# Two of the weight tiles of a Strassen product in the buffers of x, and the plain block second

## The chip, the cores and the metric

The kernel runs on one core of a Trainium2 chip. The time is device microseconds of one execution, and the median of several runs counts. The core has a matrix engine (TensorE, PE in the profile, with PEld for its loads of the stationary operand), a vector engine (VectorE, DVE), a scalar engine (ScalarE, ACT), a general engine (GpSimd, POOL) and a sequencer that here only issues transfers (SyncE, SP). Each engine works through its own list of instructions in order and waits on semaphores for the others. Transfers are issued from SP's list or from POOL's.

## The reference: what is computed

A decoder trunk of two layers on 256 tokens of width 1024, in float32. Each layer runs a SwiGLU, a token mixer and a second SwiGLU, each followed by a layer norm of `ALPHA * x + ...`. The four SwiGLUs are what matters here:

```
def _swiglu(x, w1, w3, w2):
    return (jax.nn.silu(x @ w1) * (x @ w3)) @ w2
...
        h = _swiglu(x, ffn_w1[l, 0], ffn_w3[l, 0], ffn_w2[l, 0])
        x = _layernorm(ALPHA * x + 0.5 * h, ln_g[l, 0], ln_b[l, 0])
```

The hidden width is 2816, so the last product, `h @ w2`, has 256 rows, 2816 terms and 1024 columns. There are four such products, the w2 stages of this text.

## The kernel before, in words

**Arithmetic.** Every float32 operand is split into a rounded part "hi" and the rest "lo" (ACT copies hi, DVE subtracts to get lo), and a product is three matmuls: hi by hi, hi by lo, lo by hi. Weights come from memory as raw float32 chunks of 128 x 2048 (1 MB) into a pool of four buffers (`raw_pool`, `RAW = 4`), are split in halves of 1024 columns into the pools `hi` and `lo` (eight buffers each), and are read by PE from there. `fetch` (its transfer is L161 of the profile) takes a raw buffer and issues the load on SP. `stream` is fetch and split (ACT L183, DVE L185); `split` is a split of its own (ACT L225, DVE L227).

**A SwiGLU.** `ffn` computes h in pieces. Blocks of 512 columns come in token order (`gemm_b2`), and each half is turned over by POOL's copies (L198), a transpose by DMA that SP issues (L202) and POOL's joining copies (L207); then ACT and DVE split it (L743, L745). Two column tiles come last in transposed order (`gemm_a2`, PE lines L261, L273 and L280). The input x lies in two tiles of a pool `xs` with two buffers; the last matmul that reads them is that of L280, just before the w2 stage. The norm behind the stage takes the same two buffers for the new x.

**The w2 stage** is `gemm_seven`. Of h, the first 8 of 22 column tiles form 2 x 2 blocks, and so do the matching rows of w2, in two column halves: w11, w21, w12, w22, each one chunk of 1 MB. This part is computed by a variant of Strassen's algorithm with seven block products; the names S1, S2 and so on in this text are the sums of weight blocks. The other 14 rows of tiles of w2 go through plain matmuls. `product` (PE L360) is one block product, 12 matmuls. `between` puts a group of 12 plain matmuls (PE L375) between two products; `rest` streams the chunks for it. The first column half is done in these groups; the second column half follows as a block behind them, first for the first 128 tokens, then for the others.

The sums of weight blocks are made in place. `plus` (DVE L344) adds a block to the raw tile r1: r1 = w11, then w11 + w12, then that + w22. `gather` (L339) lets a transfer of POOL's queue add a block from memory to a raw tile: to r2 (w12 + w22) and at the end to r1. So the raw tiles r1, r2 and, until its own product, r3 = w22 stay held while rest chunks and w21 come through the same pool. The results of the products are folded into the token rows `xtok` by DVE (`fold`, L573); two products share a bank with a fold in between, so the second has to wait for the fold.

**Order.** PE's list is written out by hand, in the order of the calls. For the other engines a planner orders the instructions by priority: `step()` in `fetch` and `gather` raises the number for what follows, and the planner can move an instruction that waits for a late one behind others. In its order of SP, the transposes of the last blocks of h stand among the loads of the w2 stage. `ffn` makes the object `Norm`, whose constructor asks for the norm's weights on POOL's queue (`bc_load`, L540) and, unless it is the last, for the two new x tiles.

Of the kernel before, what the change touches and what calls it, by code (L numbers as in the profile page):

```python
# [11 lines left out]
F32 = mybir.dt.float32  # L12
# [8 lines left out]
P = 128  # L21
# [15 lines left out]
CH = 2048  # L37
# [17 lines left out]
def trunk(ctx, tc, x, xT, w13a, w13b, w2, wb, wqk, wu, wg, wgr, wbr, wbrr, wo, gateb, gatebr, sgug, sgub, sguwT, sgubias, lam, diffg,  # L55
# [6 lines left out]
    raw_pool = ctx.enter_context(tc.tile_pool(name="raw", bufs=RAW))  # L62
    hi_pool = ctx.enter_context(tc.tile_pool(name="hi", bufs=HL))
    lo_pool = ctx.enter_context(tc.tile_pool(name="lo", bufs=HL))
    xs = ctx.enter_context(tc.tile_pool(name="xs", bufs=2))
# [8 lines left out]
    def name(s):  # L74
        serial[0] += 1
        return f"{s}_{serial[0]}"

    def bank():
        return psum.tile([P, 512], F32, tag="main", name=name("bank"))

    def side_bank():
        return psum.tile([P, 512], F32, tag="side", name=name("sbank"))
# [26 lines left out]
    def step():  # L109
        chunk[0] += 1  # L110
        tc.cur_priority = chunk[0] * STEP
# [12 lines left out]
    def beat(w):  # L124

        clock[0] += w
        for task in list(tasks):
            if task[0] <= clock[0]:
                turn(task)
# [18 lines left out]
    def behind(ins):  # L148

        return tc.issue_after(ins) if ins is not None else nullcontext()  # L150

    def fetch(src, width=CH):

        step()
        raw = raw_pool.tile([P, CH], F32, tag="raw", name=name("raw"))
        for g in gate:
            g[0] -= 1
        while len(gate) > 1 and gate[1][0] < 0:
            gate.pop(0)
        with behind(gate[0][1] if gate and gate[0][0] < 0 else None):  # L160
            loaded[0] = nc.sync.dma_start(raw[:, :width], src).ins  # L161
        return raw

    def stream(src, width=CH, sub=HC, lent=(), after=(None, None), pool=()):

        raw = fetch(src, width)
        out = []
        first = sooner.pop() if sooner else latest  # L170
        for o in range(0, width, HC):
            eng = G if o // HC in pool else V
            if o // HC in lent:
                hi, lo = ([act.tile([P, 512], F32R, tag="slot", name=name(n)) for _ in range(2)] for n in ("lhi", "llo"))
                at = [(hi[j], lo[j]) for j in range(2)]
            else:
                hi = hi_pool.tile([P, HC], F32R, tag="hi", name=name("whi"))
                lo = lo_pool.tile([P, HC], F32R, tag="lo", name=name("wlo"))
                at = [(hi[:, p : p + sub], lo[:, p : p + sub]) for p in range(0, HC, sub)]
            for p, (h, w) in zip(range(0, HC, sub), at):  # L180
                r = raw[:, o + p : o + p + sub]
                with behind(first[0]):
                    A.activation(h, r, AF.Copy)  # L183
                with behind(after[o // HC] or (first[1] if eng is V else None)):
                    eng.tensor_tensor(out=w, in0=r, in1=h.bitcast(F32), op=ALU.subtract)  # L185
            out.append((hi, lo))
        return out
# [35 lines left out]
    def split(hi, lo, src, eng=V, after=(None, None)):  # L223
        with behind(after[0]):
            a = A.activation(hi, src, AF.Copy).ins  # L225
        with behind(after[1]):
            return a, eng.tensor_tensor(out=lo, in0=src, in1=hi.bitcast(F32), op=ALU.subtract).ins  # L227
# [91 lines left out]
                    rows_b(ps, t, k, piece, xh, xl, kts, o, n)  # L319
                done(t, ps[:, :n], o, n)  # L320

    def gemm_seven(src, xh, xl, sums, ln, done):

        q = [[bank(), bank()], [side_bank(), bank()]]
        bx, bz = side_bank(), q[1][0]
        (w11, w21), (w12, w22) = ([s[:, o : o + CH] for o in (0, CH)] for s in src)

        def gather(raw, more):
            step()
            for o in range(0, CH, HC):
                G.dma_start(raw[:, o : o + HC], more[:, o : o + HC], accum_op=ALU.add)  # L339
            return raw  # L340

        def plus(raw, more):
            for o in range(0, CH, HC):
                V.tensor_tensor(out=raw[:, o : o + HC], in0=raw[:, o : o + HC], in1=more[:, o : o + HC], op=ALU.add)  # L344
            return raw

        def pieces(raw):
            out = []
            for o in range(0, CH, HC):
                hi = hi_pool.tile([P, HC], F32R, tag="hi", name=name("whi"))  # L350
                lo = lo_pool.tile([P, HC], F32R, tag="lo", name=name("wlo"))
                split(hi, lo, raw[:, o : o + HC])
                out.append((hi, lo))
            return out

        def product(ps, x, w, start, stop):
            for k in range(4):
                hi, lo = (v[:, k % 2 * 512 : k % 2 * 512 + 512] for v in w[k // 2])
                for n, (y, o) in enumerate(((hi, 0), (lo, 0), (hi, 1))):
                    PE.matmul(ps, x[o](k), y, start=start and k == n == 0, stop=stop and k == 3 and n == 2,  # L360
                              skip_group_check=True)
                beat(0.25)

        def rest(c):
            for k in range(8, FT, 4):
                nk = min(4, FT - k)
                for j, piece in enumerate(stream(src[c][:, k * 512 : (k + nk) * 512], nk * 512)):
                    yield k + 2 * j, piece

        def rows(t, c, k0, piece, o=0, n=512):  # L370
            for j in range(2):
                k = k0 + j
                hi, lo = (w[:, j * 512 + o : j * 512 + o + n] for w in piece)
                for m, (y, x) in enumerate(((hi, xh), (lo, xh), (hi, xl))):
                    PE.matmul(q[c][t][:, :n] if o == 0 else more[:, :n], x(k)[:, t * P : (t + 1) * P], y,  # L375
                              start=k == 8 and m == 0 and (c, t) != (1, 0), stop=k == FT - 1 and m == 2, skip_group_check=True)
            beat(n / 1024)

        def block(t, k0):
            return tuple(lambda k, f=f: f(k0 + k)[:, t * P : (t + 1) * P] for f in (xh, xl))  # L380

        a11, a12, a22 = block(0, 0), block(0, 4), block(1, 4)
        first = rest(0)

        def between():
            k, piece = next(first)
            for t in range(NT):
                rows(t, 0, k, piece)

        r1 = fetch(w11)  # L390
        product(bx, a11, pieces(r1), True, False)
        ln.fold(0, 0, bx, ALU.add, True)
        r2 = fetch(w12)
        between()
        product(bz, sums[0], pieces(plus(r1, r2)), True, False)
        ln.fold(1, 1, bz, ALU.add, True)
        r3 = fetch(w22)
        between()
        product(bx, sums[1], pieces(plus(r1, r3)), False, False)
        ln.fold(0, 1, bx, ALU.subtract, True)  # L400
        between()
        product(bz, sums[3], pieces(r3), False, False)
        between()
        product(q[0][0], a12, pieces(fetch(w21)), False, False)
        between()
        product(bx, sums[2], pieces(gather(r2, w22)), False, False)
        ln.fold(1, 1, bx, ALU.subtract, False)
        between()
        product(bx, a22, pieces(gather(r1, w21)), False, True)
        ln.fold(1, 0, bx, ALU.add, True)  # L410
        between()
        for t in range(NT):
            done(t, q[0][t], 0, 512)
        held = list(rest(1))
        cuts = ((0, 512),), (((0, 256), (256, 256)) if ln.last else ((0, 512),))
        for t in range(NT):
            for o, n in cuts[t]:
                more = bank() if o else None
                for k, piece in held:
                    rows(t, 1, k, piece, o, n)  # L420
                done(t, (more if o else q[1][t])[:, :n], 512 + o, n)
# [288 lines left out]
    def ffn(l, f, i, norm, last=False):  # L710
        xh, xl = parts(both)
        h_hi = [act.tile([P, 512], F32R, tag="slot", name=name("hhi")) for _ in range(FT // 2)]
        h_lo = [act.tile([P, 512], F32R, tag="slot", name=name("hlo")) for _ in range(FT // 2)]
        hh, hl = view(h_hi), view(h_lo)
# [35 lines left out]
        held, sums = {}, []  # L750
# [27 lines left out]
        for j in range(FA, FT - 4, 2):  # L778
            for m, z in gemm_a2([w13a[l, f, j - FA + m] for m in range(2)], both, lambda m: t512("silu")):
                s = z[:, :T]  # L780
                silu[0] = A.activation(s, s, AF.Silu).ins
                V.tensor_tensor(out=s, in0=s, in1=z[:, T:], op=ALU.mult)
                split(hh(j + m), hl(j + m), s)
        ln = Norm(l, i, 2.0 * ALPHA, 4.0 * EPS, s[:, :1], last)

        def done(t, p, c, n):
            ln.part(t, c, p, True)
            if c + n == D:
                ln.finish(t, 1.9)

        gemm_seven([w2[l, f, c] for c in range(2)], hh, hl, sums, ln, done)
        return ln.close()

    def mixer(l, i, norm):
# [388 lines left out]
```

## Time and profile before

| what | value |
|---|---|
| median of 3 runs | 1233.44 us (1230.58 to 1237.23) |
| profiled execution, time | 1224.23 us |
| profiled execution, span of the trace | 1222.5 us |
| mean granted clock of PE in it | 0.994 |
| busy: PE, DVE, ACT, POOL | 1200.6, 964.6, 745.0, 365.1 us |
| read from memory | 244.91 MB |
| w2 stages begin at | 125.19, 544.38, 731.75 and 1150.84 us |

The profiled execution is one of its own, 9.2 us below the median of the runs. In the timeline a row gives start, length, engine, line, operation, tiles (written <- read), count and, in brackets, the idle time ahead of it and what ended that; adjacent rows of the same kind are merged. In the view of waits a row gives who waited for whom, the total, how often, and the longest. A matmul's length in a row overlaps the next one, since matmuls are pipelined; the pace is seen from start to start. Transfer rows give what was loaded, count, size and the time from issue to landing.

### The profile page before, as it was taken

How to read it: one execution, taken by the hardware profiler on the slowest of the kernel's cores; microseconds unless marked ns; L12 is line 12 of the kernel's file. 1: busy time of each engine (PE TensorE's matmuls, PEld its weight loads, DVE VectorE, ACT ScalarE, POOL GpSimd, SP SyncE). 2: the span in 40 equal slices, each digit the busy share in tenths (PEclk: the TensorE clock that was granted, in tenths of full speed). 3: DMA queues.
4: the chain of work that ended last, by engine and by line, in shares of the span. 5: the costliest groups of instructions: out<-in, count | busy, mean ns of one | idle time of the engine just before them, and what ended most of it. 6: DMA issues, size and time to landing. Idle time of an engine off the chain costs nothing. (4 is left out here: it accounts for less than half of the span.)

```text
span 1222.5 us, 16873 instructions
## 1 busy us (share of the span) xinstructions
PE 1200.6 (98%) x5819; PEld 1005.2 (82%) x5819; DVE 964.6 (79%) x1632; ACT 745.0 (61%) x1424; POOL 365.1 (30%) x458
## 2 busy tenths in 40 slices
PE   9999999999999999998999999999999999999988
PEld 8888788888888888886788887788888888888867
DVE  7677789897688976776896777988966989776776
ACT  7475567668865655554664655676788556654561
POOL 1425101256411232431052351003564012324300
PEclk9999999999999999998999999999999999999999
DMA  9958786667765577695776686776675764775781
GB/s 347 322 163 263 183 308 203 260 195 225 237 219 183 184 239 233 190 229 170 289 232 203 196 254 184 282 258 242 205 211 198 250 191 155 267 246 164 207 273 37
DMA packets 126310, 271.97 MB, mean 222 GB/s; under 512 B 88672, under 2 KB 89744, under 8 KB 100112
## 3 DMA queue, kind: packets, MB, share of 16 engines
q1 hardware_dynamic: 119664, 248.80, 61.5%
q0 software_dynamic: 6128, 21.57, 7.5%
q8 instruction: 45, 0.74, 0.2%
q10 hardware_dynamic: 432, 0.52, 0.1%
q14 instruction: 41, 0.34, 0.1%
HBM read 244.91 MB, written 1.05 MB: 201 GB/s over the span
## 5 line engine op out<-in xcount | busy, mean ns | idle before, releaser
L185 DVE TENSOR_TENSOR wlo<-raw,whi 128x512 fp32r<-128x512 f32 (+1 forms) x534 | 474.7, 927 | 56.2 <-ACT whi L183 38.6
L183 ACT ACTIVATE whi<-raw 128x512 fp32r<-128x512 f32 (+1 forms) x538 | 396.3, 782 | 169.0 <-PE bank L261 92.3
L261 PE MATMUL bank<-whi,x 128*128 128x512 f32 x1480 | 460.1, 390 | 0.0
L261 PEld LDWEIGHTS bank<-whi,x 128*128 128x128 f32 x1480 | 277.9, 188 | 57.4
L261 PE MATMUL bank<-wlo,x 128*128 128x512 f32 x740 | 288.0, 389 | 0.0
L198 POOL COPY planes<-planes 128x512 uint16<-128x512 uint16 x80 | 110.1, 1404 | 211.6 <-DVE planes L724 208.9
L261 PEld LDWEIGHTS bank<-wlo,x 128*128 128x128 f32 x740 | 139.0, 188 | 28.5
L273 PE MATMUL bank<-x,whi 128*128 128x512 f32 x640 | 153.3, 391 | 0.0
L273 PEld LDWEIGHTS bank<-x,whi 128*128 128x128 f32 x640 | 118.2, 188 | 23.8
L227 DVE TENSOR_TENSOR wlo<-raw,whi 128x1024 fp32r<-128x1024 f32 (+1 forms) x72 | 77.6, 1113 | 37.1 <-ACT whi L225 25.2
L225 ACT ACTIVATE whi<-raw 128x1024 fp32r<-128x1024 f32 (+1 forms) x72 | 66.4, 956 | 53.8 <-DMA raw<-in_w 30.2
L724 DVE TENSOR_TENSOR planes<-planes,bank 128x512 f32<-128x512 f32 x40 | 27.4, 684 | 76.0 <-issue 61.1
L723 ACT ACTIVATE planes<-bank 128x512 f32<-128x512 f32 x40 | 23.8, 596 | 99.7 <-PE bank L261 97.1
L280 PEld LDWEIGHTS bank<-x,wlo 128*128 128x128 f32 x640 | 81.4, 191 | 2.9
L280 PE MATMUL bank<-x,wlo 128*128 128x256 f32 x640 | 82.6, 283 | 0.0
L375 PE MATMUL bank<-whi,hhi 128*128 128x512 f32 (+1 forms) x182 | 68.6, 377 | 0.0
L375 PE MATMUL bank<-wlo,hhi 128*128 128x512 f32 (+1 forms) x182 | 68.3, 375 | 0.0
L375 PE MATMUL bank<-whi,hlo 128*128 128x512 f32 (+1 forms) x182 | 67.9, 373 | 0.0
L686 POOL COPY nvia<-ntwo 128x256 uint16<-128x256 uint16 x20 | 9.9, 541 | 184.2 <-DMA ntwo<-nvia 166.6
L818 POOL TENSOR_TENSOR swap<-swap,sin_t 128x512 f32<-128x512 f32 x16 | 27.6, 1724 | 99.6 <-DMA swap<-z 48.3
L207 POOL COPY planes<-planes 128x512 uint16<-128x512 uint16 x48 | 38.5, 841 | 45.3 <-DMA planes<-planes 45.2
L281 ACT ACTIVATE r<-bank 128x256 f32<-128x256 f32 x96 | 34.7, 371 | 21.7 <-PE bank L280 21.7
(243 smaller groups left out, 1836.5 us busy)
## 6 DMA issues: line engine op xcount, KB each, us to landing
raw<-in_w13b SPq DMA_DIRECT2D x76, 1024.0 KB, 5.8
raw<-in_w SPq DMA_DIRECT2D x40, 1024.0 KB, 6.1
raw<-in_wb SPq DMA_DIRECT2D x16, 1024.0 KB, 6.0
raw<-in_wqk SPq DMA_DIRECT2D x16, 1024.0 KB, 6.3
raw<-in_w13a SPq DMA_DIRECT2D x8, 1024.0 KB, 5.1
raw<-in_w POOLq DMA_DIRECT2D x16, 512.0 KB, 7.3
raw<-in_wgr SPq DMA_DIRECT2D x8, 1024.0 KB, 5.2
raw<-in_wg SPq DMA_DIRECT2D x8, 1024.0 KB, 5.0
```

Source lines behind the costliest of these rows:

```text
L183: A.activation(h, r, AF.Copy)
L185: eng.tensor_tensor(out=w, in0=r, in1=h.bitcast(F32), op=ALU.subtract)
L198: G.tensor_copy(out=planes(out)[:, w], in_=numbers(src)[:, w])
L207: eng.tensor_copy(out=numbers(out)[:, w], in_=planes(src)[:, w])
L225: a = A.activation(hi, src, AF.Copy).ins
L227: return a, eng.tensor_tensor(out=lo, in0=src, in1=hi.bitcast(F32), op=ALU.subtract).ins
L261: PE.matmul(ps, xx, w, start=start and n == 0, stop=stop and n == 2)
L273: PE.matmul(b[-1], hi[:, k * P : (k + 1) * P], xc(k), start=k == 0, stop=False)
L280: PE.matmul(b[n][:, :T], lo[:, k * P : (k + 1) * P], xc(k)[:, :T], start=False, stop=k == KT - 1)
L281: emptied[0] = A.activation(r[:, s], b[n][:, T:], AF.Copy, scale=scale).ins
L375: PE.matmul(q[c][t][:, :n] if o == 0 else more[:, :n], x(k)[:, t * P : (t + 1) * P], y, start=k == 8 and m == 0 and (c, t) != (1, 0), stop ...
L818: turned_by[0] = G.tensor_tensor(out=s3, in0=s3, in1=s, op=ALU.mult).ins
```

## The change

Three things change in `gemm_seven` and around it. The tiles r2 (w12) and r3 (w22) are no longer taken from the raw pool but from the pool of x (`spare`), whose two buffers are idle during the stage; `fetch` gets an argument for that. The plain product of the block w21 (B21), which was the fifth, becomes the second, so that w21 is fetched early and w12 and w22 later. And the new x tiles of the norm are taken from the pool after the spare ones. The number of products, matmuls, additions and loads stays the same.

```diff
-    def fetch(src, width=CH):
+    def fetch(src, width=CH, raw=None):
 
         step()
-        raw = raw_pool.tile([P, CH], F32, tag="raw", name=name("raw"))
+        if raw is None:
+            raw = raw_pool.tile([P, CH], F32, tag="raw", name=name("raw"))
...
-    def gemm_seven(src, xh, xl, sums, ln, done):
+    def gemm_seven(src, xh, xl, sums, spare, ln, done):
...
         r1 = fetch(w11)
         product(bx, a11, pieces(r1), True, False)
         ln.fold(0, 0, bx, ALU.add, True)
-        r2 = fetch(w12)
+        between()
+        product(q[0][0], a12, pieces(fetch(w21)), False, False)
+        r2, r3 = (fetch(w, raw=v) for w, v in zip((w12, w22), spare))
         between()
         product(bz, sums[0], pieces(plus(r1, r2)), True, False)
         ln.fold(1, 1, bz, ALU.add, True)
-        r3 = fetch(w22)
         between()
         product(bx, sums[1], pieces(plus(r1, r3)), False, False)
         ln.fold(0, 1, bx, ALU.subtract, True)
         between()
         product(bz, sums[3], pieces(r3), False, False)
-        between()
-        product(q[0][0], a12, pieces(fetch(w21)), False, False)
         between()
         product(bx, sums[2], pieces(gather(r2, w22)), False, False)
         ln.fold(1, 1, bx, ALU.subtract, False)
...
+        spare = [xs.tile([P, 4, 512], F32, tag="x", name=name("spare")).rearrange("p k c -> p (k c)") for _ in range(2)]
         ln = Norm(l, i, 2.0 * ALPHA, 4.0 * EPS, s[:, :1], last)
...
-        gemm_seven([w2[l, f, c] for c in range(2)], hh, hl, sums, ln, done)
+        gemm_seven([w2[l, f, c] for c in range(2)], hh, hl, sums, spare, ln, done)
```

## The prediction

> **What bounds the kernel now.** I read the page first: its span and the busy time of TensorE (PE).
>
> ```profile
> span 1222.5 us, 16873 instructions
> PE 1200.6 (98%) x5819; PEld 1005.2 (82%) x5819; DVE 964.6 (79%) x1632; ACT 745.0 (61%) x1424; POOL 365.1 (30%) x458
> ```
>
> PE is idle for 1222.5 - 1200.6 = 21.9 us in all. The view of who waited for whom, for PE alone, says where:
>
> ```profile
> PE bank L360 <- ACT whi L225: 5.4, 3, 2.2
> PE sbank L360 <- ACT whi L225: 4.2, 1, 4.2
> PE bank L360 <- DVE wlo L227: 3.0, 4, 0.8
> PE sbank L360 <- DVE wlo L227: 1.8, 3, 0.8
> PE sbank L360 <- DVE xtok L573: 1.7, 2, 1.1
> ```
>
> These five rows are 16.1 us, and all stand before L360, `product` in the four w2 stages. Nearly every stall of PE lies in the code that the change touches. The stages as stretches of time (stretch, length, PE busy, matmuls touched, granted clock, DMA share, GB/s), then the pace of full-speed matmuls:
>
> ```profile
> 125.19:184.58 59.39, 56.87 (x242) 0.97 0.73 241
> 544.38:608.60 64.22, 57.56 (x242) 0.95 0.73 223
> 731.75:791.01 59.26, 55.65 (x242) 1.00 0.72 242
> 1150.84:1205.00 54.16, 50.72 (x213) 0.97 0.55 168
> 114.10 7.42 PE L273 MATMUL bank<-x,whi 128*128 128x512 f32 x32
> 121.36 4.00 PE L280 MATMUL bank<-x,wlo 128*128 128x256 f32 x32
> ```
>
> The pace is (121.36 - 114.10) / 32 = 0.227 us a matmul. The first three stretches hold 240 matmuls that start in them (7 products and 7 groups of `between` of 12, 42 for the first row block of the second half, 30 of the other), the last one 210. At the pace that is 54.5 and 47.6 us, so the stages lose 4.9, 9.7, 4.8 and 6.5 us: **25.9 us**, the most the change can win. I number the fourteen groups of 12 matmuls (2.72 us each) g0 to g13. The loss in stage 1 sits at g8, the product with B21, in the timeline of PE:
>
> ```profile
> 136.10 0.39 PE L360 MATMUL sbank<-whi,sum 128*128 128x512 f32 x1
> 149.18 0.50 PE L360 MATMUL bank<-whi,hhi 128*128 128x512 f32 x1 [1.76 <-ACT whi L225]
> 150.44 0.50 PE L360 MATMUL bank<-wlo,hhi 128*128 128x512 f32 x1 [0.76 <-DVE wlo L227]
> 152.38 0.63 PE L360 MATMUL bank<-wlo,hhi 128*128 128x512 f32 x1
> 152.81 0.63 PE L360 MATMUL bank<-whi,hlo 128*128 128x512 f32 x1
> 559.61 0.80 PE L360 MATMUL sbank<-whi,sum 128*128 128x512 f32 x1 [4.16 <-ACT whi L225]
> 756.31 0.50 PE L360 MATMUL bank<-whi,hhi 128*128 128x512 f32 x1 [2.23 <-ACT whi L225]
> ```
>
> Up to g4 (136.10) the stage runs at pace. g8 comes 1.76 us late, its second matmul 0.76 more, and after that the pace falls to 152.81 - 152.38 = 0.43 us for about eight matmuls, some 1.6 us more. Stage 3 (756.31) stalls at g8 too, stage 2 (559.61) at g4. What g8 waits for, on ACT, DVE, SP and in the DMA:
>
> ```profile
> 148.07 1.06 ACT L225 ACTIVATE whi<-raw 128x1024 fp32r<-128x1024 f32 x1 [7.93 <-DMA raw<-in_w]
> 140.28 0.34 SPq L161 DMA_DIRECT2D raw<-in_w  x1
> 139.03 1.22 DVE L185 TENSOR_TENSOR wlo<-raw,whi 128x1024 fp32r<-128x1024 f32 x1
> ```
>
> w21 is issued only at 140.28, when DVE has read the last of another chunk at 139.03 + 1.22, and is in ACT's hands 7.8 us later. Four raw buffers hold w11, w12 and w22 for long, so one is left for all else. That is the wait that the change takes away.
>
> **The change part by part.** *Same work.* The matmuls, splits, additions and bytes are the same. B21 moves from g8 to g2; the sums of S1, S2 and the product with w22 move from g2, g4, g6 to g4, g6, g8.
>
> *w21 early.* It takes the raw buffer that w12 had before, is loaded before the stage and is needed at g2, so the wait at g8 goes. Its price: the two rows of waits with the tile bank are g8's alone, 5.4 + 3.0 = 8.4 us idle; each of the 7 waits costs about 0.25 more at the restart (150.44 - 149.18 is 1.26 where the wait is 0.76 and the pace 0.23); the slow pace comes behind g8 in stages 1 and 4 (clock 0.97; 1.00 in stage 3), 1.6 each. In all 13.4 us. What g8 needs instead, w22, is asked for some 21 us earlier.
>
> *The transposes move forward on SP.* SP's order now has w11, w12, a rest chunk, w22, a rest chunk, then the two transposes of the last column block of h; afterwards it has w11, rest, w21, rest, the transposes, rest, and only then w12 and w22 into the x buffers. The accumulating loads of w12's buffer by POOL move behind the transposes as well.
>
> ```profile
> 118.25 0.33 SPq L161 DMA_DIRECT2D raw<-in_w  x1
> 118.62 1.28 SPq L202 DMA_TRANSPOSE planes<-planes  x1
> 539.26 0.86 POOL L339 DMA_DIRECT2D raw<-in_w  x1 [1.38 <-DVE raw L344]
> 129.17 1.46 POOL L207 COPY planes<-planes 128x512 uint16<-128x512 uint16 x2 [1.93 <-DMA planes<-planes]
> 553.96 0.76 POOL L207 COPY planes<-planes 128x512 uint16<-128x512 uint16 x1 [7.55 <-DMA planes<-planes]
> 131.42 0.43 DVE L227 TENSOR_TENSOR hlo<-silu,hhi 128x256 fp32r<-128x256 f32 x1 [2.10 <-ACT hhi L225]
> 132.42 2.35 DVE L344 TENSOR_TENSOR raw<-raw,raw 128x1024 f32<-128x1024 f32 x2
> ```
>
> The first transpose stood behind a load that had to wait until 118.25, and both ran beside an accumulating load (539.26). The second landed at 129.17 and, in stage 2, at 553.96; ACT waits for it in order, DVE for ACT (131.42), and the addition for g4 behind that (132.42). This chain ends in stage 2's stall of 4.16 us; the two rows of waits with sbank on ACT and DVE, 6.0 us, are its cost in stages 2 and 4, and with restarts and slow pace (clock 0.95 in stage 2) some 9 us. With the transposes ahead and the accumulating loads later, I take it to end before the stage's fourth microsecond. If it does not, that is the third rival.
>
> *New: w12 lands late.* The x buffers come free when PE has done its last L280 matmul, at the start of the stage (125.19; with the matmul's own time 125.5). Then w12 is issued, and the addition r1 + w12 for g4 waits for it. Loads of 1 MB, with the time from issue to landing in us as the last number: one alone (issued 521.28); the second of a pair issued 0.6 us apart (709.26); and one with two accumulating loads ahead (746.95):
>
> ```profile
> raw<-in_w SPq DMA_DIRECT2D x1, 1024.0 KB, 5.2
> raw<-in_w SPq DMA_DIRECT2D x1, 1024.0 KB, 7.2
> raw<-in_w SPq DMA_DIRECT2D x1, 1024.0 KB, 8.1
> 135.03 2.35 DVE L227 TENSOR_TENSOR wlo<-raw,whi 128x1024 fp32r<-128x1024 f32 x2
> 137.30 0.68 DVE L573 SCALAR_TENSOR_TENSOR xtok<-xtok,sbank 128x512 f32<-128x512 f32 x1
> ```
>
> I take 5.2, since the queue ahead of w12 should be near empty: 130.7. DVE itself is free at about that time: in the trace its wait for ACT begins at 131.42 - 2.10 = 129.3, and two hlo, a copy and a fold, some 1.4 us, stand between there and the addition: 130.7. Call it S. From S, DVE works in order: the addition, two passes (2.27; 135.03 - 132.42 less the hlo between), an hlo (0.34), two splits for g4 and two for g5 (4 x 1.135, the step of the rows of two), the second addition (2.27), a fold (0.60) and the first split for g6 (1.14): 11.2 us. g6 needs that split at its second matmul, 125.19 + 73 x 0.227 = 141.8. So g6 waits S + 11.2 - 141.8 = **0.1 us**, and g4 none (S + 3.8 = 134.5 against 136.3). I take 0.5, for the x-buffer semaphore and for POOL's broadcasts of the norm's weights in the same stretch. Bounds: 0, and 3.0 with the 8.1 row.
>
> *Later in the stage* DVE goes on without a gap: from S to the fold that frees the bank for g12 there are 26.7 us by the same steps; g12 would start at 125.19 + 144 x 0.227 = 157.9, the fold ends at 157.4. Of the accumulating loads into r1, the second is issued about 143 and its landing can hold up the splits in front of that fold:
>
> ```profile
> raw<-in_w POOLq DMA_DIRECT2D x16, 512.0 KB, 7.3
> raw<-in_w POOLq DMA_DIRECT2D x1, 512.0 KB, 10.0
> 586.72 0.47 PE L360 MATMUL sbank<-whi,hhi 128*128 128x512 f32 x1 [1.08 <-DVE xtok L573]
> ```
>
> (the first row is the median of all sixteen). With 10.0 us it lands at 153, which makes the fold about 2 us late; with 7.3, nothing. Between 0 and 2 I take 0.7, near the 1.08 that stage 2 already shows at this place.
>
> *The sum.* Each stage then loses 0.5 + 0.7 + 0.3 (small delays that stand in all four now) = 1.5 us, 6.0 in all, against 25.9: a gain of **20 us**. The profiled execution, 1224.23 us, would become 1204; it is 9.2 us under the median of the runs, 1233.44, and I take the gain from that median: **1213 us**.
>
> *The clock.* The rows show a slow pace after idle times of 1.76 + 0.76 us (152.38), yet stage 3 kept a clock of 1.00 with 2.23. The Trainium skill (TensorE: Matmul & The Clock Gate, "What's actually happening") says that the clock falls only after an idle window of about 3.4 us, free-running. By that rule stalls like these cost no clock, and 1.6 us of stage 1's loss would need another cause; the trace disagrees with its number (0.97 mean clock in stage 1, whose longest idle time is 1.76 us). My sum needs no such loss afterwards by either.
>
> **The rivals.** *Second: DVE is the bound, fed late (0.20).* If w12 lands after 7.2 us, as the second of a pair, S is 132.7 and g6 waits 2.1 us; with 1.6 of slow pace and 0.3 that is 4.0 a stage, 16 in all: 1233.4 - 10 = 1223. For it: a rest chunk is issued just ahead and POOL's two 512 KB broadcasts fall into the same microseconds. Against: the rest chunk should be issued some 5 us earlier. The Trainium skill (DMA: Bandwidth & Descriptors, "Queues, rings and completion order") says that each DMA engine takes turns between queues by packets; by that rule the broadcasts do delay w12, which would be this case. No row here shows the two together without something else.
>
> *Third: the transposes stay late (0.10).* Then DVE's chain starts at 132.4 as now, but with one addition more in front of g6: 132.4 + 11.2 - 141.8 = 1.8 us a stage, and the losses at g4 in stages 2 and 4 stay. The gain is 13.4 - 4 x 1.8 = 6.2: 1227, just about no change (0.5% of 1233.44, 6.2 us, is what a measurement of this kernel can tell).
>
> *Fourth, slower: w12 lands far too late (0.08).* The transpose and the accumulating load that ran together in stage 2 took this long:
>
> ```profile
> raw<-in_w POOLq DMA_DIRECT2D x1, 512.0 KB, 14.3
> planes<-planes SPq DMA_TRANSPOSE x1, 14.7
> ```
>
> If w12 fell into such a time, 14 us, S would be 139.5, g6 late by 8.9, with 1.9 of slow pace and small delays 10.8 a stage: 43 against 25.9, 1251. It decides from 6.5 us a stage on, that is a wait of 4.6, S = 135.2, a landing of 9.7 us. Against: no plain load of 1 MB in these rows is over 8.1.
>
> **How the numbers follow.** First case 0.62, the others as given. Faster by over 0.5%: 0.62 + 0.20 + a third of the third case, 0.85; within 0.5%: 0.08; slower: 0.07. The range reaches from all 25.9 us won, counted from the lowest run before (1230.58 - 25.9 = 1204.7), to the third case: 1204 to 1227; the likeliest case alone is 1206 to 1220.
>
> **What would show it.** In the waits of PE, no L360 wait on ACT at g8 in any stage. The transposes issued before the last rest chunk, and POOL's second joining copy before the stage's first microseconds are over. The loads into the spare buffers issued within 0.5 us of the last L280 and landed within 5 to 6. PE's wait at g6 under 1 us on a wlo, at g12 under 2 on xtok. Stage lengths of about 56 us to the same point (now 59.4, 64.2, 59.3), clock 1.00. Wrong would be: a long wait at g4 or g6 on DVE's addition, idle DVE in front of L344 until the spare load lands, or new idle time behind the stage, where loads of the next weights follow.

## The result, and the profile after

| kernel | median | lowest to highest | runs |
|---|---|---|---|
| before | 1232.15 us | 1230.58 to 1237.23 | 4 |
| after | 1199.78 us | 1198.79 to 1202.38 | 4 |

The ratio is 0.973, with an interval from 0.970 to 0.977: 32.4 us less. The prediction was faster, at 1213 us with a range of 1204 to 1227, so the direction was right and the time lies 4 us below the range. The profiled execution took 1198.81 us.

The span and the first line of busy times on the page of the changed kernel:

```profile
span 1197.1 us, 16880 instructions
PE 1191.1 (100%) x5819; PEld 1002.1 (84%) x5819; DVE 958.4 (80%) x1632; ACT 745.9 (62%) x1424; POOL 363.0 (30%) x458
```

Its view of who waited for whom, for PE alone (total, how often, longest):

```profile
PE sbank L492 <- DVE warm L488: 1.1, 1, 1.1
PE sbank L623 <- ACT minus L621: 0.7, 1, 0.7
PE bank L480 <- ACT whi L226: 0.3, 1, 0.3
```

Line numbers are one higher than before, so `product` is L361 now, and no row names it: the view has no wait of PE in the four w2 stages (the trace has one gap of 0.15 us there, at the second matmul of g6 in stage 4). Between the two profiled executions the span fell by 25.4 us. Of that, 15.9 is idle time of PE (1222.5 - 1200.6 = 21.9 before, 6.0 now) and 9.5 is busy time (1200.6 to 1191.1), which is the slower pace and the restarts behind the waits. The stages as stretches, with the columns of the same view before:

```profile
125.16:179.75 54.59, 54.59 (x242) 1.00 0.82 270
539.57:594.00 54.43, 54.43 (x242) 1.00 0.83 270
717.15:771.65 54.50, 54.50 (x243) 1.00 0.83 270
1131.47:1179.56 48.09, 47.94 (x213) 1.00 0.66 197
```

At the pace of 0.227 us, 240 and 210 matmuls are 54.5 and 47.6 us. The first three lose at most 0.1 us, the last one 0.5 (at that gap of g6): all but 0.5 us of the 25.9 is won, and the stages stand at the bound of the matmuls. The steps of the prediction in the timelines of POOL, SP, DVE and PE, stage 1:

```profile
121.27 1.44 POOL L208 COPY planes<-planes 128x512 uint16<-128x512 uint16 x2 [1.47 <-DMA planes<-planes]
131.64 1.81 POOL L340 DMA_DIRECT2D spare<-in_w  x2 [1.53 <-DVE raw L345]
124.87 0.81 SPq L162 DMA_DIRECT2D spare<-in_w  x2
129.87 2.36 DVE L345 TENSOR_TENSOR raw<-raw,spare 128x1024 f32<-128x1024 f32 x2
139.88 1.22 DVE L228 TENSOR_TENSOR wlo<-raw,whi 128x1024 fp32r<-128x1024 f32 x1
157.04 0.68 DVE L573 SCALAR_TENSOR_TENSOR xtok<-xtok,sbank 128x512 f32<-128x512 f32 x1
157.87 0.47 PE L361 MATMUL sbank<-whi,hhi 128*128 128x512 f32 x1
```

And the first load into a spare buffer in the view of transfers:

```profile
spare<-in_w SPq DMA_DIRECT2D x1, 1024.0 KB, 4.8
```

POOL's second joining copy stands at 121.27 (129.17 before), so the transposes are no longer late. The spare load is issued at 124.87 and lands at 129.7. DVE comes to the addition at 129.87 without any idle time in front of it: the load was in time by 0.2 us. The first split for g6 stands at 139.88 and is done at 141.1, and the fold for g12 is done at 157.7, just before PE starts g12 at 157.87.

### The profile page after: what moved, and what is told of

It is laid out like the page before. It is cut to its first block, busy times and chain, and to the rows that moved or that the text cites. A ratio compares the mean times of both kernels' runs of the same rounds, so it can differ in the third digit from the quotient of the medians.

```text
span 1197.1 us, 16880 instructions
## 1 busy us (share of the span) xinstructions
PE 1191.1 (100%) x5819; PEld 1002.1 (84%) x5819; DVE 958.4 (80%) x1632; ACT 745.9 (62%) x1424; POOL 363.0 (30%) x458
## 4 chain that ended last, share of the span: by engine, by line
PE 98%; DVE 1%; DMA 1%; ACT 0%; issue 0%; ACTq 0%
PE bank L262 53%; PE bank L274 15%; PE bank L376 9%; PE bank L281 8%; PE sbank L361 5%; PE sbank L376 3%; PE bank L480 2%; PE sbank L843 1%; PE bank L361 1%; PE sbank L899 1%; PE sbank L1017 1%; DMA bc<-in_lng 0%; PE sbank L897 0%; DMA xraw<-in_xT 0%; DVE wlo L186 0%; PE sbank L644 0%
## 5 line engine op out<-in xcount | busy, mean ns | idle before, releaser
L262 PEld LDWEIGHTS bank<-wlo,x 128*128 128x128 f32 x740 | 138.9, 188 | 28.3
L228 DVE TENSOR_TENSOR wlo<-raw,whi 128x1024 fp32r<-128x1024 f32 (+1 forms) x56 | 58.5, 1071 | 26.9 <-issue 18.4
L226 ACT ACTIVATE whi<-raw 128x1024 fp32r<-128x1024 f32 (+1 forms) x56 | 52.0, 937 | 42.5 <-DVE raw L345 18.8
```

Source lines behind the costliest of these rows:

```text
L262: PE.matmul(ps, xx, w, start=start and n == 0, stop=stop and n == 2)
```

## The experiments

Time lost in stages, below, is the length of the four stages less their matmuls at 0.227 us each.

**The kernel before, once more.** The median of before was 9.2 us above its profiled execution. What a slower execution of it loses, and where, was open. No edit.

> The kernel before, unchanged, for its spread: its profiled execution took 1224.2 us at a mean granted clock of 0.994, its timed ones 1230.6 to 1237.2. Theory A (the clock): the timed executions lose more to slow pace behind the same stalls; then their mean granted clock is lower, about 0.988 at 1231 us and 0.983 at 1237 us, and time and clock go together over the runs. Theory B (the waits): transfers land later in them and PE waits longer; then the clock stays within 0.002 of 0.994 while the times differ by 6 to 13 us. Theory C: time outside the span; then time minus span is some 8 us instead of 1.7.

Measured: 1231.88 us (1227.25 to 1236.33). Its profiled execution took 1231.40 us, at a clock of 0.992. The longest waits of PE:

```profile
PE sbank L360 <- ACT whi L225: 12.7, 3, 5.9
...
PE bank L360 <- ACT whi L225: 0.6, 1, 0.6
```

The first row, stalls at g4, was 4.2 us in one stage in the profile that the prediction rests on; here it is 12.7 in three. The last one, w21's wait at g8, was 5.4 there and is 0.6 here. What the two executions differ in is the landing of the last transposes. Stage 2 in the timelines of PE and POOL:

```profile
559.34 0.79 PE L360 MATMUL sbank<-whi,sum 128*128 128x512 f32 x1 [5.59 <-ACT whi L225]
553.71 1.42 POOL L207 COPY planes<-planes 128x512 uint16<-128x512 uint16 x2 [8.91 <-DMA planes<-planes]
```

The transfers issued in the same microseconds:

```profile
raw<-in_w POOLq DMA_DIRECT2D x1, 512.0 KB, 16.2
planes<-planes SPq DMA_TRANSPOSE x1, 16.2
```

The transpose and the accumulating load beside it both take 16.2 us, and stage 3 shows the same stall (5.88 us at 748.71). The stages lose 3.2, 11.4, 11.6 and 6.9, together 33.1 us, where the first profile lost 25.9: 7.2 us more, as much as the two executions lie apart. This execution took 1231.4; less 33.1 that is 1198.3, within 0.5 us of the changed kernel's profiled execution and 1.5 of its median. So what the change wins in a typical execution is all that such an execution loses in its stages. The time outside the span is 1.7 us in both profiles (1231.4 - 1229.7, 1224.23 - 1222.5), so theory C falls; the difference lies in these waits and in the slow pace behind them. Theory A asked for a clock of 0.988 at 1231 us and 0.983 at 1237, and the runs show 0.992 at 1231.40 and at 1236.33. Theory B has the mechanism, though the clock did not stay within its 0.002: over the twelve runs it lies between 0.989 and 0.996.

**The order alone.** B21 second, w12 and w22 in the raw pool:

```diff
-        r2, r3 = (fetch(w, raw=v) for w, v in zip((w12, w22), spare))
+        r2, r3 = (fetch(w) for w in (w12, w22))
```

> The block B21 second, but w12 and w22 in raw buffers as before. My theory (what held w21 back was the shortage of raw buffers at the fifth product, so the order alone removes that wait): no wait at g8; w12 and w22 are loaded ahead of the stage, the transposes stand behind them on SP, so the late transposes of stages 2 and 4 stay and g4 waits there as before; about 10 us of the 32 stay lost: 1208 to 1215 us. Rival (both parts are needed, since four raw buffers are still held by w11, w12, w22 and one chunk): waits of 2 to 4 us a stage move to another group, 1220 to 1230 us.

Measured: 1220.48 us (1212.0 to 1229.47), ratio 0.993 (0.989 to 0.996). The longest of PE's waits:

```profile
PE sbank L361 <- DVE xtok L573: 13.1, 3, 6.2
```

SP and POOL in stage 1, in the timeline:

```profile
128.64 0.34 SPq L162 DMA_DIRECT2D raw<-in_w  x1
129.09 7.85 SPq L203 DMA_TRANSPOSE planes<-planes  x2
142.67 1.44 POOL L208 COPY planes<-planes 128x512 uint16<-128x512 uint16 x2 [11.85 <-DMA planes<-planes]
```

No wait for w21 is left, as the prediction has it: w21 early is the work of the order. But with w12 and w22 held in the four raw buffers from early on, SP's transposes stand behind a load that cannot be issued before 128.64, and POOL joins the last of them only at 142.67. What DVE does behind them is late, up to 6.2 us at g12. The landing adds to that. Of the transfers issued between 129.4 and 131.2 us:

```profile
bc<-in_lnb POOLq DMA_DIRECT2D x1, 512.0 KB, 12.3
planes<-planes SPq DMA_TRANSPOSE x2, 13.2
```

The accumulating loads are not what these transposes had beside them, since the second of those landed at 129.3 (121.53 + 7.8), 0.2 us after the first transpose was issued. POOL's two plain broadcasts of the norm's weights were, and a load of 1 MB issued at 128.64. The time is well above the 1208 to 1215 that the theory expected, and at the lower end of the range of the view that the buffers are needed too. Its runs spread over 17.5 us, more than those of the kernel before.

**The buffers alone.** B21 stays fifth, w12 and w22 go into the spare buffers:

```diff
-        r2 = fetch(w12)
+        r2 = fetch(w12, raw=spare[0])
...
-        r3 = fetch(w22)
+        r3 = fetch(w22, raw=spare[1])
```

> w12 and w22 in the buffers of x, but B21 the fifth product as before. My theory: w12 is needed at g2, 5.4 us into the stage, and is issued only at its start, so DVE's addition begins at 4.7 us and the split for the second matmul of g2 ends at 8.2 us where it is wanted at 5.7: a wait of about 2.5 us at g2 in every stage, some of it with slow pace, and none at g8: 1210 to 1218 us. Rival (the order does nothing, the buffers are all): no wait over 0.5 us in any stage, 1199 to 1203 us.

Measured: 1221.39 us (1218.51 to 1222.96), ratio 0.993 (0.990 to 0.995). The waits of PE:

```profile
PE sbank L361 <- ACT whi L226: 11.4, 4, 4.8
PE sbank L361 <- DVE wlo L228: 2.7, 4, 0.8
```

The first of them in the timelines of SP, DVE and PE:

```profile
125.02 0.81 SPq L162 DMA_DIRECT2D spare<-in_w  x2
131.47 2.36 DVE L345 TENSOR_TENSOR raw<-raw,spare 128x1024 f32<-128x1024 f32 x2 [1.39 <-DMA spare<-in_w]
133.90 0.50 PE L361 MATMUL sbank<-whi,hhi 128*128 128x512 f32 x1 [2.97 <-ACT whi L226]
```

Waits at g8, g4 and g12 are gone; in their place each stage waits at g2. There S1 is wanted 5.4 us after the stage's start, and its spare buffer is free only at that start. The place was as expected, the size larger: 24.0 us lost in stages, of which the waits are 14.1. So the order is what gives the spare load its time: B21 second is the cover under which w12 lands.

**One tile in a spare buffer, order as before.** w22 in a spare buffer, w12 in the raw pool:

```diff
-        r3 = fetch(w22)
+        r3 = fetch(w22, raw=spare[0])
```

> Only w22 goes into a buffer of x, w12 stays in a raw buffer, B21 stays fifth. w22 is needed first at g4, 10.9 us into the stage. My theory: one raw buffer more in the ring is enough for w21, so the wait at g8 goes; the transposes stand ahead of w21's load on SP, so g4 is fed by DVE from 4.7 us on and does not wait: 1199 to 1204 us, like the changed kernel. Rival (both buffers and the new order are needed): g8 still waits more than 1 us on ACT for w21, 1210 us or more.

Measured: 1206.09 us (1204.66 to 1208.57), ratio 0.981 (0.978 to 0.983). The waits of PE in the stages:

```profile
PE sbank L361 <- DVE xtok L574: 5.4, 4, 2.2
...
PE sbank L361 <- DVE wlo L228: 0.4, 1, 0.4
```

The longest one in its timeline, with the next matmul:

```profile
577.17 0.47 PE L361 MATMUL sbank<-whi,hhi 128*128 128x512 f32 x1 [2.17 <-DVE xtok L574]
577.48 0.39 PE L361 MATMUL sbank<-wlo,hhi 128*128 128x512 f32 x1
```

One buffer more for the raw pool takes away most of the loss: no wait for w21, next to none at g4 (the second row), and only the fold for g12 is late. The time came 2 us above the expectation. After a single wait of 2.17 us the pace is nearly at once the usual one (577.48 - 577.17 is 0.31), and the clock of this execution is 1.00.

**The accumulating load later, nothing else.** The kernel before, with one edit: POOL issues the accumulating loads into w12's tile behind the broadcasts of the norm's weights, so behind its last joining copies. The lists of SP, DVE, ACT and PE are unchanged:

```diff
-                G.dma_start(raw[:, o : o + HC], more[:, o : o + HC], accum_op=ALU.add)
+                with behind(spread[0]):
+                    G.dma_start(raw[:, o : o + HC], more[:, o : o + HC], accum_op=ALU.add)
```

> The kernel before with one difference: the accumulating load into w12's buffer is put behind the norm's broadcasts on POOL's queue, so that it no longer runs beside the last two transposes; orders on DVE, ACT and SP are the same. Theory D (the accumulating load makes the second transpose late, 13 to 15 us instead of 8.7, and in how many stages it does so differs from one execution to the next, which is what the timed runs before paid beyond the profiled one): the second transpose lands within 9 us in all four stages, PE's waits at g4 go to under 1 us each, the waits at g8 stay or grow by a microsecond, since the accumulating loads now run nearer to w21's; 1214 to 1222 us, and the spread over the runs halves. Rival E (the load of 1 MB on SP right ahead of the transposes makes them late): the second transpose still takes 13 us or more in one to three stages, time within 4 us of before.

Measured: 1226.41 us (1225.73 to 1227.57), ratio 0.998 (0.996 to 1.000). The longest of PE's waits:

```profile
PE bank L361 <- ACT whi L225: 11.7, 4, 3.5
```

g8 of stage 1 in the timeline:

```profile
150.61 0.50 PE L361 MATMUL bank<-whi,hhi 128*128 128x512 f32 x1 [3.48 <-ACT whi L225]
```

No wait at g4 is left in any stage, and the longest landing of a transpose fell from 14.7 to 8.6 us. The spread of its times is 1.8 us over 12 runs, against 11.5 us over 22 runs of the kernel before beside it. So the late transposes of the kernel before, and its spread with them, come from the accumulating load beside them. The time fell less than expected. All four stages now wait for w21 at g8, for up to 3.5 us: it is asked for about as late as before (139.76 in stage 1, 140.28 before), and with the accumulating loads now in its time it lands after 9.6 us instead of 7.7.

That a transpose and an accumulating load run beside each other is not the whole condition. In stage 1 of the first profile of before, the pair issued between 120.0 and 120.6 us shows

```profile
raw<-in_w POOLq DMA_DIRECT2D x1, 512.0 KB, 8.1
planes<-planes SPq DMA_TRANSPOSE x1, 8.6
```

So do stage 3 of that profile (8.0 and 8.7) and stage 1 of the second one (8.1 and 8.6). In these three the load was issued 0.15 to 0.37 us ahead of the transpose; in the other five stages of the two profiles it came 0.09 to 0.13 us behind it, and the transpose took 13.4 to 16.3 us. Whether this order is the cause was not tried.

**The spare loads made late.** The changed kernel, but each spare buffer gets one column written by DVE behind the first fold, which its load has to wait for:

```diff
+        for v in spare:
+            V.tensor_copy(v[:, :1], ln.y[0][:, :1])
         r2, r3 = (fetch(w, raw=v) for w, v in zip((w12, w22), spare))
```

> The changed kernel, but the loads into the x buffers wait, through a copy of one column by DVE into each, for the first fold: they are issued some 4.5 us into each stage instead of at its start. The prediction's step for DVE's chain: the addition starts about 10.2 us into the stage, g4 waits 2.9 us and g6 the rest, together 4.8 to 5.3 us a stage, with 1.6 us of slow pace in some: 1219 to 1227 us. Rival (the chain has more slack than its sum says, because in the changed kernel almost no wait was left): under 2 us a stage, below 1208 us.

Measured: 1237.15 us (1236.34 to 1237.32), ratio 1.006 (1.004 to 1.007). The longest of PE's waits:

```profile
PE sbank L361 <- ACT whi L226: 19.3, 6, 5.6
```

Stage 1 in the timelines of SP, DVE and PE:

```profile
130.31 0.80 SPq L162 DMA_DIRECT2D spare<-in_w  x2
138.89 1.23 DVE L345 TENSOR_TENSOR raw<-raw,spare 128x1024 f32<-128x1024 f32 x1 [7.59 <-DMA spare<-in_w]
141.32 0.80 PE L361 MATMUL sbank<-whi,hhi 128*128 128x512 f32 x1 [4.87 <-ACT whi L226]
```

The transfers of the same microseconds:

```profile
spare<-in_w SPq DMA_DIRECT2D x2, 1024.0 KB, 9.5
bc<-in_lng POOLq DMA_DIRECT2D x1, 512.0 KB, 5.0
bc<-in_lnb POOLq DMA_DIRECT2D x1, 512.0 KB, 7.0
```

The issue is 5.4 us later and the addition 9.0 (138.89 for 129.87), since the load now meets the two broadcasts and takes 8.6 us to the addition. The stages lose 38.7 us. That is more than the expectation's 1219 to 1227 allows, which had 5.7 us from the issue to the addition (10.2 - 4.5), and it makes the kernel slower than before. The fourth rival's turning point, S = 135.2, agrees with this: S = 138.9 lies behind it and the time is on the other side. No run lies near the point itself.

**The changed kernel, once more.**

> The changed kernel, unchanged, beside more runs of the kernel before on the same chip. If its waits do not depend on when transposes land, its runs lie within 4 us of each other, at 1199 to 1203 us, where the kernel before spreads over 8 to 12 us; the ratio to before lies between 0.972 and 0.976.

Measured: 1199.84 us (1199.42 to 1200.92), ratio 0.976 (0.973 to 0.979), as expected: its five runs spread over 1.5 us, the 22 of the kernel before beside it over 11.5.

**One tile in a spare buffer, with the new order.** The changed kernel with w12 in the raw pool again:

```diff
-        r2, r3 = (fetch(w, raw=v) for w, v in zip((w12, w22), spare))
+        r2, r3 = fetch(w12), fetch(w22, raw=spare[0])
```

> The changed kernel with only w22 in a buffer of x; w12 goes into the raw pool again, still after w21 in the calls. With this run the table of order (B21 fifth or second) by number of tiles outside the pool (0, 1, 2) is full. So far: old order 1231, 1206, 1221; new order 1220, ?, 1200 us. Theory (what counts is when SP can issue the transposes and what they run beside): w12 stands ahead of the transposes on SP again and the accumulating load into its tile beside them, so the transposes of stages 2 to 4 land late in some executions; no wait at g8, waits at g4, g6 or g12 behind DVE, 2 to 5 us in the worst stages, 1203 to 1215 us, and a wider spread of its times than the changed kernel's 1.5 us. Rival (one tile less in the pool is all that is wanted, whichever the order): no wait over 1 us, 1199 to 1203 us, as the changed kernel. A second rival (with B21 second the fold ahead of g12 is late, as in the run of the order alone, whatever the transposes do): waits of 5 to 6 us at g12 in several stages, 1215 to 1222 us.

Measured: 1231.03 us (1227.41 to 1234.78), ratio 1.000 (0.998 to 1.003): all three expectations missed. The longest of PE's waits:

```profile
PE sbank L361 <- ACT whi L226: 20.5, 4, 8.1
```

DVE's second addition in stage 1, in the timeline:

```profile
144.42 2.36 DVE L345 TENSOR_TENSOR raw<-raw,spare 128x1024 f32<-128x1024 f32 x2 [9.53 <-DMA spare<-in_w]
```

The transfers issued between 118 and 126 us:

```profile
raw<-in_w POOLq DMA_DIRECT2D x2, 512.0 KB, 21.2
spare<-in_w SPq DMA_DIRECT2D x1, 1024.0 KB, 19.4
planes<-planes SPq DMA_TRANSPOSE x2, 13.2
```

The stretch from 130 to 136 us in the view of windows (length, busy times of PE, PEld, DVE, ACT and POOL with their instructions, then clock, DMA share and GB/s):

```profile
130.00:136.00 6.00, 6.00 (x28) 4.99 (x27) 4.89 (x5) 0.10 (x1) 0.00 (x0) 1.00 1.15 79
```

Again the transposes run beside the accumulating loads and are late (POOL's last joining copies begin at 139.19), in stage 1 also with the load issued first, by 0.05 us, and a second one behind it. What the theory had not counted is the plain load of w22: issued at 124.89 into the same time, it lands only after 19.4 us, and g6, which needs r1 + w22, waits in every stage, up to 8.1 us.

**The same with the accumulating load later.** One edit to the kernel just told, the one of `gather` shown above; the lists of SP, DVE, ACT and PE stay as they are.

> The kernel of the run before (B21 second, only w22 in a buffer of x), with one edit: the accumulating loads into w12's tile stand behind the broadcasts of the norm's weights on POOL's queue, instead of ahead of POOL's last two joining copies. Theory (the transposes and the plain load into the buffer of x are slow because the accumulating loads run beside them): the transposes land within 9 us, POOL's last joining copies stand at about 129 instead of 139, w22's load into the buffer of x lands within 5 to 8 us of its issue instead of 19.4, the waits at g6, 20.5 us in the four stages, are gone, and the time falls from 1231 to 1199 to 1206 us. Rival (the transposes and the plain load of the buffer of x get in each other's way without any accumulating load, since they are issued within 5 us of each other): landing 12 us and more still, waits at g6 of over 2 us in most stages, 1215 to 1231 us.

Measured: 1201.43 us (1200.91 to 1202.69), ratio 0.974 (0.972 to 0.977), some 30 us less than without the edit. The same views, one by one:

```profile
PE sbank L362 <- DVE xtok L574: 1.9, 3, 0.7
```

The timeline of DVE:

```profile
136.67 2.35 DVE L346 TENSOR_TENSOR raw<-raw,spare 128x1024 f32<-128x1024 f32 x2
```

The transfers issued between 118 and 126 us:

```profile
spare<-in_w SPq DMA_DIRECT2D x1, 1024.0 KB, 6.9
planes<-planes SPq DMA_TRANSPOSE x2, 6.8
```

The stretch from 130 to 136 us:

```profile
130.00:136.00 6.00, 6.00 (x28) 4.99 (x27) 6.00 (x10) 1.41 (x3) 3.90 (x6) 1.00 0.94 299
```

The transposes land in 6.8 instead of 13.2 us, the load of w22 in 6.9 instead of 19.4, and the additions stand at 136.67 with no idle time ahead of them. The DMA engines are counted as occupied in both stretches (1.15 and 0.94), but move 79 GB/s in the one and 299 in the other. The rival, that the transposes and the plain load alone get in each other's way, falls. In both runs with this edit nothing of POOL's queue is left beside the last transposes, the broadcasts included, so they do not tell an accumulating load from another load of that queue.

All medians together (those of the kernel before lay between 1229 and 1233 us beside these runs); the column on the right has the accumulating loads into w12's tile behind POOL's last joining copies by the edit above:

| tiles outside the raw pool | B21 fifth | B21 second | with the edit of `gather` |
|---|---|---|---|
| none | 1231 (before) | 1220 | 1226 (B21 fifth) |
| w22 | 1206 | 1231 | 1201 (B21 second) |
| w12 and w22 | 1221 | 1200 (after) | not run |

## Why the prediction was wrong, and where it was right

The direction and the mechanism were right. Two steps failed. The sum charged each stage 1.5 us, 6.0 in all, and the stages lost 0.5 in all; and the gain, worked out inside one execution, was taken off the median of others that lose more. With the first alone put right the forecast is 1233.4 - 25.4 = 1208, still inside the range; the second put the time below it.

*What bounds the kernel* was right: the stages' loss is what the change could win, and it won all but 0.5 us. Nothing new appeared behind the stages.

*w21 early* was right as a mechanism: no run with B21 second waits for w21 anywhere, whatever else it waits for. That w22 is needed only at g8 was a slip: S2 at g6 contains it, so it has until DVE's second addition (137.02 in stage 1), and landed 3.5 us ahead of that (125.35 + 8.2).

*The transposes move forward* was right in its result: POOL's last joining copies are done 2.4 us before the stage begins (121.27 + 1.44 against 125.16), and DVE has no idle time ahead of the addition. It named both causes, the load that SP's transposes stood behind and the accumulating load beside them. The runs separate them: moving the accumulating loads alone removes every wait at g4 of the kernel before, and the same edit is worth 30 us with B21 second and w22 in a spare buffer. In the changed kernel nothing had to be moved on POOL's list by hand: w12 comes into a buffer that is free only at the stage's start, and its accumulating load, which follows DVE's first addition, is issued at 131.64 in stage 1, when the transposes are long done. That is what the spare buffers do beside giving room in the pool.

*w12 lands late* was sized too high, but nearly exact in its steps. Landing: predicted 5.2 us, measured 4.8. S: predicted 130.7, measured 129.87. From S to the split for g6: predicted 11.2, measured 11.2 (141.1 - 129.87). g6 needed it at 141.8 by the prediction, and 141.73 is when PE has it. The wait of 0.1 us that this chain gives is what shows in stage 4 (0.15, at g6's second matmul, on DVE's split); the 0.5 us put in its place did not come in the other three.

*Later in the stage*: the fold for g12 was put at 157.4 with g12 at 157.9, and ends at 157.7 with g12 at 157.87. The 0.7 us on top did not come, nor did the 0.3 of small delays. So of the 1.5 us a stage, "6.0 in all", 0.5 in all was left. This is the first step that failed, by 5.5 us. Without it, 1204 for the profiled execution becomes 1224.23 - 25.4 = 1198.8, and 1198.81 was measured.

*The base* is the second, and with 9.2 us the larger one: "it is 9.2 us under the median of the runs, 1233.44, and I take the gain from that median". The gain came from an execution that lost 25.9 us, the start from executions that lose more. The second profile of before shows an execution at 1231.4 us, 7.2 slower than the first, that lost 33.1, 7.2 more, most of it behind the late transposes of stages 2 and 3. Where a change takes away the cause of a spread, the slow executions gain more than the quick ones and all end at one floor: 1224.23 - 25.9 and 1231.4 - 33.1 are both 1198.3. The low end of the range, "counted from the lowest run before (1230.58 - 25.9 = 1204.7)", has the same fault; worked out inside the one execution it would have been 1198. The spread was in sight beforehand: the profiled execution was 6 us quicker than the lowest of the three runs, and the prediction did not ask which wait made the difference.

*The rivals.* The second, w12 as the second of a pair, did not come: w12 was the first of the two spare loads, at 4.8 us, and the 8.2 of the second had time. The third did not come in the changed kernel. The run with B21 second and w12 alone in the raw pool has late transposes, and its 1231 is worse than the rival's 1227, but what it waits for is w22's late load. The fourth was made to happen by the late spare loads, with S = 138.9: 38.7 us lost for its 43 at S = 139.5, and slower than before. Its argument "no plain load of 1 MB in these rows is over 8.1" was weaker than it looked, since the same load took 19.4 us beside transposes and accumulating loads. And the change had little to spare: by stage 1 of its profile, an estimate, a landing more than 0.8 us later (0.2 until DVE has to wait, 141.73 - 141.10 until g6 does) would have begun to cost, and in stage 4 g6 already waits.

*The clock.* That no slow pace would be left was right (0.999). The Trainium skill (TensorE: Matmul & The Clock Gate, "What's actually happening") ties the lower clock to an idle window of about 3.4 us. The runs agree with a plain reading of that only in part: the pace fell behind waits of 1.76 + 0.76 us with one matmul between, and not behind a single wait of 2.17 us. The sum of the waits does not decide it either: behind 2.23 + 0.76 us in stage 3 of the kernel before the pace stayed at 0.23 us a matmul and the clock at 1.00, while stage 3 of the run with the buffers alone, with 1.72 + 0.76 us, has a mean clock of 0.94. What decides it stays open.

## What to carry to other kernels

When a change removes the cause of a spread, take the floor inside one execution (its time less what it loses), and do not carry its gain over to the median of others. Before moving a tile to another buffer, look at which transfers its new moment of issue keeps apart: here one tile in a spare buffer gave 1206, 1231 or 1201 us, and between the last two the only edit is when the accumulating loads are issued. And two parts of a change can each win a third and need each other: a buffer that comes free late needs an order that gives its load time. A smaller part can also win most of it: w22 alone in a spare buffer, in the old order, won 25 of the 32 us.

## What the hardware showed that was not expected

A transpose by DMA that has loads of 512 KB of POOL's queue beside it can take far longer than their bytes explain. Beside accumulating loads the last transpose took 13 to 19 us in nine stages of twelve (three profiles), and 6 to 8 us with the same loads moved behind it; a plain load of 1 MB issued into that stretch took 16.5 to 19.4 us in the four stages, and 4.8 to 6.9 without. In that stretch the DMA engines count as occupied and move 79 GB/s. How long it takes varies from one execution to the next, and in the kernel before this makes up the spread: 11.5 us with it, 1.8 without.

It does not always happen, and accumulating is not needed for it. In the other three of the twelve stages, all of the kernel before, the same pair took 8 to 9 us; and in the run of the order alone the transposes of stage 1 took 13.0 and 13.5 us with plain broadcasts of POOL's queue beside them. Nor is it shown that the transposes slow the accumulating loads: with none beside them, in the run where they come later, those took 8.0 to 17.6 us. Why the transfers disturb each other, the traces do not show.
